# Identity products between token tiles, and the affine map that writes the rounded operand, in the first stage of a two-layer hybrid backbone

## The chip, the cores and the metric

The kernel runs on one core of a Trainium2 chip. Its five engines each work through a queue of their own: TensorE (matmuls and transposes, "PE" in the profile, with "PEld" its weight loads), VectorE ("DVE"), ScalarE ("ACT"), GpSimd ("POOL") and SyncE ("SP", which here only starts DMA transfers). Matmuls read SBUF and write PSUM; VectorE and ScalarE read both memories; GpSimd is used on SBUF alone here. The metric is the device time of one execution in microseconds (us).

## What is computed

Two layers over 512 latent tokens and 256 context tokens of width 1024. Every sub-layer normalises its input, modulates it, mixes it and adds it back:

```python
m_lat = jnp.split((sc @ mod_w[l] + mod_b[l])[:, None, :], 6, axis=-1)
m_ctx = jnp.split((scc @ mod_w[l] + mod_b[l])[None, None, :], 6, axis=-1)
h_ctx = _modulate(_rms(x_ctx, norm_pre_mix[l]), m_ctx[0], m_ctx[1])
h_lat = _modulate(_rms(x_lat, norm_pre_mix[l]), m_lat[0], m_lat[1])
...
def _rms(x, gain, eps=1e-6):
    xf = x.astype(jnp.float32)
    y = xf * lax.rsqrt(jnp.mean(xf * xf, axis=-1, keepdims=True) + eps)
    return (y * gain.astype(jnp.float32)).astype(x.dtype)
...
def _modulate(h, shift, scale):
    return h * (1 + scale) + shift
```

Here `sc` and `scc` are silu of the condition vectors, and `mod_w[l]` has 1024 rows and six column blocks of 1024. Layer 0 then projects h with `even_w_in`, runs gated linear attention beside grouped-query attention, projects the result out and applies a SwiGLU feed-forward; layer 1 does the same with an HGRN2 mixer. The change concerns only what comes first: norm and modulation of layer 0, and the first columns (288 of them: gate inputs and part of the queries) of its input projection.

## The kernel before

**Operands in two parts.** Large matmuls run on a rounded type (fp32r in the profile). To keep f32 accuracy each operand is split into H, the value rounded, and L, the remainder of value minus H, and a product is three matmuls (`mm3`): H by H, H by L, L by H. In most places ScalarE writes H as a cast and VectorE writes L as a subtraction (`put`, line 740, the operand x; `fetched`'s `split`, line 781, the weights wH and wL).

**The order.** A scheduler lays the instructions of each engine's queue in an order at build time, by priority in the text and by what it estimates to be ready. Instructions of TensorE that are made while `self.pinned` is set keep the order of the text. `issue_after(x)` adds an edge that keeps what is made inside it, where it is on x's own engine, behind x in that queue; other engines are not held. `behind()` (line 1543) does this for every instruction in `self.latest`. An engine works through its queue in order.

**The first stage**, in `run` (lines 1918 to 2037), is written out by hand:

- `constants` (line 373) makes the identity on GpSimd, starts the DMAs of some rows of constants on ScalarE's queue, and turns them with one transpose (pt_rows) into columns (col). From these ScalarE makes scT, silu of the conditions.
- `fetch` and `loads` start all the transfers on SyncE's queue: the six token tiles xt (two of context, 4 and 5, then four latent, 0 to 3), then for each quarter qd of the model width eight pieces of mod_w (mraw, 256 KB each, nine double-piece buffers) and 288 columns of the input projection (zraw).
- `turn(t)`, once for each token tile: ScalarE squares and sums (junk), VectorE makes ms, GpSimd raises it to -1/2 (rs), VectorE scales the tile in place (xt, line 1931), TensorE transposes its eight 128x128 blocks into a PSUM tile of which there are two buffers (line 358, xT), and ScalarE and VectorE copy one half each into xT in SBUF (line 1938).
- `sums(qd, ks)`: the two column blocks shift and scale of the modulation, for one quarter, as f32 matmuls with scT for weights, 32 output rows at a time (mod_acc). After the second half VectorE copies the sums (modrows); `cols(qd)` transposes them (modT), adds the bias (modcol) and makes the scale with the norm's gain (aff, line 1980).
- `apply(qd, r, t0, n)`: for the two 128-row blocks k of a quarter, the affine map scale by x plus shift in place on xT, then H and L of it into the operand x. The context (r = 1, 256 tokens) goes first, then the latents (512 tokens). The map is on ScalarE for latents where k % 4 is not 0 (line 1989), and on VectorE otherwise (line 1991); the cast is on ScalarE (line 743), the remainder on VectorE (line 744).
- `weights(qd)` splits that quarter's zraw (lines 783 and 784).
- `z(t0, qd, parts)`: the projection of two token tiles over that quarter's two blocks, accumulated in PSUM (nat).

TensorE's order is: the transposes of all six tiles, both halves of quarter 0's sums; then for each next quarter: projection of the context tiles over the quarter before, half the sums, one latent tile, the other half of the sums, the second latent tile, the transpose of the sums, the last two latent tiles. The last quarter's projections are made in the mixer that follows, ahead of its own projections (gqk).

Of the kernel before, what the change touches and what calls it, by code (L numbers as in the profile page):

```python
# [8 lines left out]
F32 = mybir.dt.float32  # L9
# [3 lines left out]
AF = mybir.ActivationFunctionType  # L13
# [4 lines left out]
P = 128  # L18
D = 1024
# [297 lines left out]
class Net:  # L317
# [3 lines left out]
    def __init__(self, ctx, tc, I, out):  # L321
# [4 lines left out]
        self.pinned = False  # L326
        self.turns, self.steps, self.pair, self.casts = [], [], [], []
        pool = lambda name, bufs=1, **k: ctx.enter_context(tc.tile_pool(name=name, bufs=bufs, **k))
# [28 lines left out]
    def tr(self, *a):  # L357
        return self.pin(self.nc.tensor.transpose(*a))

    def mm_tile(self, name):  # L360
        return self.ps.tile([P, 1024], F32, tag="mm", bufs=1 if self.narrow else 2, name=name)
# [10 lines left out]
    def constants(self):  # L372
        nc, I, cst = self.nc, self.I, self.cst
        self.ident = cst.tile([P, P], F32, name="ident")
        make_identity(nc, self.ident)
        self.scT = cst.tile([P, KD, 32], F32, name="scT")
        self.neghalf = cst.tile([P, 1], F32, name="neghalf")
# [12 lines left out]
            )  # L390
        )()

        nc.gpsimd.memset(self.scT, 0.0)
# [380 lines left out]
    def fetched(self, src, k, n, raw=None):  # L774

        nc = self.nc
        raw = self.wp.tile([P, WU], F32, tag="raw", bufs=3, name="raw") if raw is None else raw
        m = k * n
        nc.sync.dma_start(out=raw[:, :m].rearrange("p (k n) -> p k n", k=k), in_=src)

        def split(pool=None, to=None):
            H, L = to or [(pool or self.wp).tile([P, WU], F32R, tag=f"w{x}", bufs=4, name=f"w{x}") for x in "HL"]
            self.casts = self.casts[-1:] + [nc.scalar.copy(H[:, :m], raw[:, :m])]  # L783
            nc.vector.tensor_tensor(L[:, :m], raw[:, :m], H[:, :m].bitcast(F32), op=ALU.subtract)  # L784
            return H[:, :m].rearrange("p (k n) -> p k n", k=k), L[:, :m].rearrange("p (k n) -> p k n", k=k)

        return split
# [1111 lines left out]
    def run(self):  # L1899
# [19 lines left out]
        with self.pool("pre0") as pp:  # L1919
# [3 lines left out]
            def fetch(*ts):  # L1923
                for t in ts:
                    xts[t] = pp.tile([P, D], F32, tag="xt", bufs=6, name=f"xt{t}")
                    nc.sync.dma_start(out=xts[t], in_=xin(t))

            def turn(t):
                xt = xts.pop(t)
                rs = self.rstd(self.sumsq(xt), D)  # L1930
                nc.vector.tensor_scalar(xt, xt, rs, None, op0=ALU.mult)
                pt = self.mm_tile(f"xT{t}")
                for k in range(KD):
                    self.tr(pt[:, k * P : (k + 1) * P], xt[:, k * P : (k + 1) * P], self.ident)
                for hf in range(2):
                    dst = xT[:, hf * 4 : hf * 4 + 4, t * P : (t + 1) * P]
                    src = pt[:, 512 * hf : 512 * hf + 512].rearrange("p (k i) -> p k i", k=4)
                    (nc.vector.tensor_copy if hf else nc.scalar.copy)(dst, src)

# [44 lines left out]
            def apply(qd, r, t0, n):  # L1984
                tok = slice(t0 * P, (t0 + n) * P)
                for k in range(2 * qd, 2 * qd + 2):
                    x = xT[:, k, tok]
                    if r == 0 and k % 4:
                        nc.scalar.activation(x, x, AF.Identity, bias=B[:, r, k : k + 1], scale=A[:, r, k : k + 1])
                    else:  # L1990
                        nc.vector.tensor_scalar(x, x, A[:, r, k : k + 1], B[:, r, k : k + 1], op0=ALU.mult, op1=ALU.add)
# [267 lines left out]
```

## Time and profile before

| | us |
|---|---|
| median of 3 runs | 1679.83 (1679.76 to 1680.23) |
| the profiled execution, whole | 1680.5 |
| its span, first to last instruction | 1678.7 |
| TensorE busy in the span | 1640.6 |
| first stage, until the last projections over the last quarter end | about 56 |

The page gives shares of the whole span; a stage is read from the chain of work that ended last (which names, step by step, what the last instruction had to wait for), from the timeline and from the table of windows. In the chain's rows the first number is the start in us, the second the length, then engine, tile and line. Line 355 is the helper of every matmul and line 358 that of every transpose, so there the tile's name tells the step.

### The profile page before, as it was taken

Reading aid. Unit: us, or ns where it says so; the run is one execution under the profiler, and the core shown is the slowest. Engines: PE = TensorE matmul, PEld = TensorE weight load, DVE = VectorE, ACT = ScalarE, POOL = GpSimd, SP = SyncE. Lnnn points to the kernel's source line nnn. Section 1 sums busy time; section 2 is a strip of 40 time slices with the busy share of each in tenths; the row PEclk is TensorE's granted clock in tenths of the full one; section 3 lists DMA queues with packets and bytes.
Section 4 is the critical chain, followed back from the end, with each engine's and each line's share of the span. In section 5 each row is a group of like instructions: output and inputs, shape, how many; then the busy total and the mean of one; then the engine's idle time right before and its main releaser. Section 6 shows DMA issues by size and latency. Waiting matters only on the chain.

```text
span 1678.7 us, 32395 instructions
## 1 busy us (share of the span) xinstructions
PE 1640.6 (98%) x13347; PEld 1476.9 (88%) x13347; DVE 1313.0 (78%) x2104; ACT 917.4 (55%) x1560; POOL 121.6 (7%) x129
## 2 busy tenths in 40 slices
PE   6999998999999999999999999999999999999997
PEld 5899987888999999998887788888888899999886
DVE  4889768866898989768668648788775599987887
ACT  4745557846544443445447536566564565555654
POOL 1004210001000000002102000000000100000310
PEclk9999999999999999999999999999999999999999
DMA  9651002164253446249516542111114334333973
GB/s 336 187 154 42 2 28 101 52 197 152 92 150 102 133 149 193 79 134 223 101 54 210 194 132 64 52 54 50 52 56 159 126 107 120 114 101 101 227 162 138
DMA packets 184735, 204.77 MB, mean 122 GB/s; under 512 B 7142, under 2 KB 141836, under 8 KB 184588
## 3 DMA queue, kind: packets, MB, share of 16 engines
q1 hardware_dynamic: 173996, 181.98, 34.6%
q0 software_dynamic: 9024, 17.30, 5.8%
q10 hardware_dynamic: 1568, 3.43, 0.6%
q8 instruction: 104, 1.70, 0.4%
q14 instruction: 43, 0.35, 0.1%
HBM read 193.23 MB, written 9.46 MB: 121 GB/s over the span
## 4 chain that ended last, share of the span: by engine, by line
PE 82%; DVE 9%; DMA 4%; ACT 4%; issue 2%; POOL 0%; DVEq 0%; ACTq 0%; POOLq 0%
PE nat L355 12%; PE a L355 10%; PE ff L355 8%; PE E L355 7%; PE x L355 6%; PE oproj L355 6%; PE o L355 4%; PE b L355 3%; PE D L355 3%; PE fq L355 3%; PE gqk L355 2%; PE pearly L355 2%; PE q L355 2%; PE S L355 2%; PE poh L355 1%
## 5 line engine op out<-in xcount | busy, mean ns | idle before, releaser
L355 PE MATMUL nat<-wH,x 128*128 128x256 f32 (+2 forms) x968 | 227.6, 322 | 2.7 <-ACT x L743 2.5
L355 PEld LDWEIGHTS nat<-wH,x 128*128 128x128 f32 x968 | 162.7, 191 | 21.2 <-ACT x L743 3.9
L840 ACT CAST wH<-raw 128x1024 fp32r<-128x1024 f32 x120 | 124.8, 1050 | 101.6 <-DVE raw L865 39.2
L841 DVE TENSOR_TENSOR wL<-raw,wH 128x1024 fp32r<-128x1024 f32 x120 | 145.7, 1221 | 24.2 <-ACT wH L840 23.7
L355 PE MATMUL nat<-wL,x 128*128 128x256 f32 (+2 forms) x484 | 153.8, 318 | 1.8 <-DVE wL L784 1.8
L784 DVE TENSOR_TENSOR wL<-raw,wH 128x1024 fp32r<-128x1024 f32 x79 | 95.7, 1222 | 50.9 <-ACT wH L783 50.0
L355 PE MATMUL ff<-x,wH 128*128 128x512 f32 (+1 forms) x512 | 127.7, 340 | 0.0
L677 POOL TENSOR_TENSOR rs<-ms,neghalf 128x1 f32<-128x1 f32 (+2 forms) x62 | 63.3, 1025 | 787.7 <-DVE ms L675 787.6
L783 ACT CAST wH<-raw 128x1024 fp32r<-128x1024 f32 x79 | 82.1, 1049 | 68.6 <-PE ff L355 19.8
L355 PE MATMUL oproj<-wH,x 128*128 128x512 f32 x320 | 102.2, 394 | 0.5 <-ACT x L1310 0.4
L355 PEld LDWEIGHTS nat<-wL,x 128*128 128x128 f32 x484 | 92.3, 191 | 7.9 <-DVE wL L784 2.7
L355 PEld LDWEIGHTS ff<-x,wH 128*128 128x128 f32 x512 | 87.3, 190 | 10.0
L606 DVE SCALAR_TENSOR_TENSOR macc<-mraw,scT,macc 128x1024 f32<-128x1024 f32 x70 | 87.9, 1280 | 9.9 <-DMA mraw<-in_mod_w_dram 9.8
L355 PE MATMUL x<-wH,two 128*128 128x512 f32 x280 | 90.5, 392 | 0.9 <-DVE y L1831 0.7
L992 ACT COPY qkh<-arr 128x512 f32<-128x512 f32 x112 | 70.1, 642 | 36.4 <-DVE arr L997 32.2
L1753 POOL DMA_DIRECT2D t<-in_ffn_w_down_dram x36 | 41.8, 1199 | 639.6 <-DVE t L1792 337.5
L355 PE MATMUL ff<-x,wL 128*128 128x256 f32 (+1 forms) x256 | 86.2, 337 | 0.0
L865 DVE TENSOR_TENSOR raw<-raw 128x512 f32<-128x512 f32 x120 | 82.7, 689 | 2.8
L997 DVE TENSOR_TENSOR arr<-arr,f 128x512 f32<-128x512 f32 x112 | 74.2, 687 | 1.9 <-ACT qkh L992 0.3
L355 PEld LDWEIGHTS oproj<-wH,x 128*128 128x128 f32 x320 | 59.9, 188 | 13.1 <-ACT x L1310 1.1
L355 PE MATMUL E<-T,wH 128*128 128x384 f32 (+1 forms) x320 | 70.3, 309 | 0.4 <-DVE go L918 0.4
L355 PE MATMUL E<-x,wH 128*128 128x384 f32 (+1 forms) x320 | 70.7, 310 | 0.0
(422 smaller groups left out, 4538.1 us busy)
## 6 DMA issues: line engine op xcount, KB each, us to landing
mraw<-in_mod_w_dram SPq DMA_DIRECT2D x80, 512.0 KB, 4.3
raw<-in_ffn_w_gate_dram SPq DMA_DIRECT2D x44, 512.0 KB, 3.8
raw<-in_ffn_w_up_dram SPq DMA_DIRECT2D x44, 512.0 KB, 4.8
raw<-in_odd_w_in_dram SPq DMA_DIRECT2D x40, 512.0 KB, 3.7
t<-in_ffn_w_down_dram POOLq DMA_DIRECT2D x30, 512.0 KB, 7.9
raw<-in_ffn_w_down_dram SPq DMA_DIRECT2D x28, 512.0 KB, 7.3
mraw<-in_mod_w_dram SPq DMA_DIRECT2D x32, 256.0 KB, 6.3
raw<-in_even_w_in_dram SPq DMA_DIRECT2D x16, 512.0 KB, 5.0
```

What stands on the lines that cost most here:

```text
L355: return self.pin(self.nc.tensor.matmul(*a, **k))
L606: nc.vector.scalar_tensor_tensor(a, u, w, a, op0=ALU.mult, op1=ALU.add)
L677: nc.gpsimd.tensor_tensor(rs, ms, self.neghalf.to_broadcast([P, w]), op=ALU.pow)
L783: self.casts = self.casts[-1:] + [nc.scalar.copy(H[:, :m], raw[:, :m])]
L784: nc.vector.tensor_tensor(L[:, :m], raw[:, :m], H[:, :m].bitcast(F32), op=ALU.subtract)
L840: self.nc.scalar.copy(H, f)
L841: self.nc.vector.tensor_tensor(L, f, H.bitcast(F32), op=ALU.subtract)
L865: add = lambda o, x, y: nc.vector.tensor_tensor(o, x, y, op=ALU.add)
L992: nc.scalar.copy(qkv[:, :, :, half, :], dst)
L997: nc.vector.tensor_tensor(dst, dst, tb, op=ALU.mult)
L1753: add = lambda o, src: self.pin(nc.gpsimd.dma_start(out=o, in_=src, accum_op=ALU.add))
```

## The change

`warm(n)` issues n f32 products of the identity with itself into a PSUM tile (idle) that nothing reads. It is called 18 times over while the constants load, and with small counts between the token tiles, around the first sums and before the first affine map; the constants' TensorE instructions are pinned now.

The norm's VectorE instructions of a token tile (ms and the scaling of xt) are put behind the VectorE half of the copy of the tile two turns earlier, from the third tile on. The last tile's turn moves behind the first half of quarter 0's sums.

`apply` no longer writes the mapped value back: ScalarE writes H straight from xT with the affine map, for every k and both streams; VectorE computes the mapped value in f32 into a spare tile (xa, four buffers) and subtracts H from it.

`weights` makes its remainder on GpSimd, for all four quarters, and quarter 0's split is put behind the last tile's copies as the others are behind the last apply.

```diff
@@ Net @@
+    def warm(self, n):
+
+        for _ in range(n):
+            self.mm(self.idle, self.ident, self.ident, start=True, stop=True)
+
@@ constants @@
         make_identity(nc, self.ident)
+        self.idle = self.sc_tile("idle", 1)[:, :P]
+        self.pinned = True
+        self.warm(18)
         self.scT = cst.tile([P, KD, 32], F32, name="scT")
...
         )()
+        self.pinned = False
@@ fetched @@
-        def split(pool=None, to=None):
+        def split(pool=None, to=None, vector=nc.vector):
...
-            nc.vector.tensor_tensor(L[:, :m], raw[:, :m], H[:, :m].bitcast(F32), op=ALU.subtract)
+            vector.tensor_tensor(L[:, :m], raw[:, :m], H[:, :m].bitcast(F32), op=ALU.subtract)
@@ run @@
+            emptied = []
+
             def turn(t):
                 xt = xts.pop(t)
-                rs = self.rstd(self.sumsq(xt), D)
-                nc.vector.tensor_scalar(xt, xt, rs, None, op0=ALU.mult)
+                ss = self.sumsq(xt)
+                with ExitStack() as behind:
+                    if len(emptied) > 1:
+                        behind.enter_context(self.tc.issue_after(emptied[-2][1].ins))
+                    nc.vector.tensor_scalar(xt, xt, self.rstd(ss, D), None, op0=ALU.mult)
...
-                    (nc.vector.tensor_copy if hf else nc.scalar.copy)(dst, src)
+                    self.latest = [*self.latest[-1:], (nc.vector.tensor_copy if hf else nc.scalar.copy)(dst, src)]
+                emptied.append(self.latest)
...
             def apply(qd, r, t0, n):
                 tok = slice(t0 * P, (t0 + n) * P)
                 for k in range(2 * qd, 2 * qd + 2):
-                    x = xT[:, k, tok]
-                    if r == 0 and k % 4:
-                        nc.scalar.activation(x, x, AF.Identity, bias=B[:, r, k : k + 1], scale=A[:, r, k : k + 1])
-                    else:
-                        nc.vector.tensor_scalar(x, x, A[:, r, k : k + 1], B[:, r, k : k + 1], op0=ALU.mult, op1=ALU.add)
-                    self.latest = self.put(h, k, tok, x)
+                    H, L = h.hl(k, tok)
+                    a, b = A[:, r, k : k + 1], B[:, r, k : k + 1]
+                    f = pp.tile([P, SEQ], F32, tag="xa", bufs=4, name="xa")[:, : n * P]
+                    cast = nc.scalar.activation(H, xT[:, k, tok], AF.Identity, bias=b, scale=a)
+                    nc.vector.tensor_scalar(f, xT[:, k, tok], a, b, op0=ALU.mult, op1=ALU.add)
+                    self.mark = nc.vector.tensor_tensor(L, f, H.bitcast(F32), op=ALU.subtract)
+                    self.latest = cast, self.mark
 
             def weights(qd):
-                if qd == 0:
-                    zu[0] = zu[0]()
-                    return
                 with self.behind():
-                    zu[qd] = zu[qd]()
+                    zu[qd] = zu[qd](vector=nc.gpsimd)
...
-            for t in order:
+            for t, n in zip(order[:-1], (1, 2, 2, 3, 3)):
                 turn(t)
+                self.warm(n)
             sums(0, lo)
+            turn(order[-1])
+            self.warm(3)
             sums(0, hi)
             weights(0)
+            self.warm(2)
             cols(0)
+            self.warm(5)
             apply(0, 1, 4, 2)
             apply(0, 0, 0, 4)
```

More of the change, by code (lines that the diff above doesn't have):

```diff
@@ L326, in __init__ @@
         self.pinned = False
-        self.turns, self.steps, self.pair, self.casts = [], [], [], []
+        self.turns, self.steps, self.pair, self.casts, self.latest = [], [], [], [], []
         pool = lambda name, bufs=1, **k: ctx.enter_context(tc.tile_pool(name=name, bufs=bufs, **k))
```

## The prediction

> **What bounds the kernel now.** The page first: which engine fills the span, and which one fills the chain of work that ended last.
>
> ```profile
> PE 1640.6 (98%) x13347; PEld 1476.9 (88%) x13347; DVE 1313.0 (78%) x2104; ACT 917.4 (55%) x1560; POOL 121.6 (7%) x129
> ...
> PE 82%; DVE 9%; DMA 4%; ACT 4%; issue 2%; POOL 0%; DVEq 0%; ACTq 0%; POOLq 0%
> ```
>
> TensorE is the bound nearly everywhere, so a microsecond saved ahead of a TensorE-bound stretch should reach the end. The change lies in the first 56 us. The chain, asked for the start of the run, in order of time (start, length, what):
>
> ```profile
> 16.33 4.47 PE xT L358 x24
> 20.80 1.93 PE mod_acc L355 x64
> ...
> 23.86 0.17 DVE aff L1980
> ...
> 24.12 0.81 ACT xT L1989
> 24.93 0.30 ACT x L743
> ...
> 25.28 2.65 PE nat L355 x12
> 27.93 1.87 PE mod_acc L355 x32
> ...
> 33.39 0.17 DVE aff L1980
> ...
> 34.75 2.04 PE nat L355 x12
> 36.80 1.01 PE mod_acc L355 x32
> ...
> 41.35 0.17 DVE aff L1980
> ...
> 46.76 1.01 PE mod_acc L355 x32
> ...
> 49.30 0.17 DVE aff L1980
> ...
> 52.84 0.70 DVE x L744
> ...
> 53.59 2.79 PE nat L355 x19
> ```
>
> Read it as one turning stage (to 20.80), the first modulation sums (to 22.73), then four quarters, each from one aff to the next. Quarter one lasts 33.39 - 23.86 = 9.53 us, the second and third 7.95 us. Quarter one is slow because the same 12 projection matmuls take 2.65 us against 2.04, and the same 32 records of sums 1.87 against 1.01. The windows view names the cause (length, busy time and count of each engine, granted TensorE clock, DMA share, GB/s):
>
> ```profile
> 26.00:26.50 0.50, 0.50 (x5) 0.50 (x5) 0.43 (x2) 0.50 (x3) 0.00 (x0) 0.97 1.08 354
> 26.50:27.00 0.50, 0.50 (x4) 0.50 (x3) 0.50 (x2) 0.50 (x2) 0.00 (x0) 0.50 1.08 348
> 29.50:30.00 0.50, 0.50 (x9) 0.28 (x2) 0.00 (x0) 0.00 (x0) 0.00 (x0) 0.62 1.10 343
> 23.06:26.47 3.41, 1.52 (x8) 1.17 (x9) 2.85 (x11) 2.35 (x5) 0.00 (x0) 1.00 1.10 360
> ```
>
> The clock stands at half from about 26.47 (0.97 in that half microsecond) to 29.88 (0.62), 3.41 us. In the 3.41 us ahead of it TensorE was busy for 1.52 us (45%): it waited for the sums' copies and the first affine map.
>
> **The turning stage.** Rows of the timeline (start, length, engine, line, in brackets the idle time before and what ended it):
>
> ```profile
> 1.30 0.29 POOL masks.py:199 TENSOR_SCALAR_AFFINE_SELECT ident<-ident 128x128 f32<-128x128 f32 x1
> ...
> 7.81 0.45 PE L358 MATMUL pt_rows<-ident,rows 128*128 128x128 f32 x1 [7.81 <-DMA rows<-in_mod_b_dram]
> ...
> 8.06 3.68 PE L358 MATMUL xT<-ident,xt 128*128 128x128 f32 x16
> ...
> 9.83 0.21 ACT L394 ACTIVATE scT<-col 128x16 f32<-128x16 f32 x1
> ...
> 11.10 0.57 ACT L1938 COPY xT<-xT 128x512 f32<-128x512 f32 x1
> ...
> 11.90 0.15 DVE L675 TENSOR_SCALAR ms<-ss 128x1 f32<-128x1 f32 x1
> ...
> 12.20 0.55 POOL L677 TENSOR_TENSOR rs<-ms,neghalf 128x1 f32<-128x1 f32 x1 [0.99 <-DVE ms L675]
> ...
> 12.78 0.75 DVE L1931 TENSOR_SCALAR xt<-xt,rs 128x1024 f32<-128x1024 f32 x1 [0.73 <-POOL rs L677]
> 13.45 0.68 DVE L1938 COPY xT<-xT 128x512 f32<-128x512 f32 x1
> ...
> 14.19 1.97 PE L358 MATMUL xT<-ident,xt 128*128 128x128 f32 x8 [2.46 <-DVE ms L675]
> ...
> 16.81 0.69 DVE L1938 COPY xT<-xT 128x512 f32<-128x512 f32 x1 [0.54 <-ACT xT L1938]
> ```
>
> The first tile's copy has ScalarE's half at 11.10 but VectorE's only at 13.45, because a later tile's norm stands ahead of it and waits 0.73 us for GpSimd. With two PSUM buffers the third tile's transposes cannot start before 14.19. One tile's eight transposes take 1.97 us there. VectorE's half starts when ScalarE's ends (16.81).
>
> What the change does here. It puts each norm behind the VectorE copy of the tile two before it, so the first copy no longer waits for norms. The cost: the norm's chain, 1.63 us from ms to the end of xt (11.90 to 13.53), now starts only after a copy. Where ScalarE's first half lands is the unknown. The transposes of that tile are the first 8 of the 16 that start at 8.06, done by 9.9, and at 10.04 ScalarE is through with two latent norms and the small scT; its row of before is 11.10, behind one more norm; behind two more it would be about 12.3. I take 10.04: first copy done at 10.04 + 0.57 + 0.69 = 11.3, third tile's transposes at 11.3 + 1.63 = 12.95. The loop over two tiles is norm 1.63, transposes, ScalarE's half 0.59, VectorE's 0.69. With transposes at full clock, about 1.2 us (below), that is 4.1 us, 2.1 a tile at least; VectorE's own work a tile, 0.15 + 0.75 + 0.69, fits beside it. So: fifth tile turned at 17.2 to 18.4, three products, first half of the sums to 20.1, last tile's transposes to 21.2 (its norm is through by 19.4), three products, second half to about 22.8. Before: 22.73. **I cost the turning stage at nothing**: the early copy and the clock pay for the norms' later start and the fillers. Ends: 1.5 us gained (products hidden, copies earlier still), 2.3 us lost (ScalarE's half at 12.3).
>
> The products' price, and the other durations, from groups that keep shapes apart (busy us in all, mean ns of one):
>
> ```profile
> L355 PE MATMUL poh<-Sh,arr 128*128 128x128 f32 x96 | 12.0, 275 | 0.0
> ...
> L1989 ACT ACTIVATE xT<-xT,modcol,aff 128x512 f32<-128x512 f32 x6 | 4.9, 814 | 17.6 <-DVE aff L1980 17.6
> ...
> L736 ACT ACTIVATE hf<-hT,modcol,aff 128x256 f32<-128x256 f32 x24 | 12.2, 557 | 1.7 <-PE hT L358 1.7
> ...
> L744 DVE TENSOR_TENSOR x<-xT,x 128x512 fp32r<-128x512 f32 x8 | 5.4, 690 | 1.6 <-ACT x L743 1.4
> ...
> L1991 DVE TENSOR_SCALAR xT<-xT,aff,modcol 128x512 f32<-128x512 f32 x2 | 1.1, 541 | 0.0
> ...
> L1362 POOL TENSOR_TENSOR natq<-natq,rs 128x512 f32<-128x512 f32 x6 | 7.7, 1289 | 15.2 <-DVE natq L1361 15.0
> ```
>
> An f32 product of 128x128x128 is two records (32 calls of the sums are 64 records at 20.80). At full clock one takes 12.0/96 = 0.125 us, so a product 0.25 us and, with its tail, eight transposes 1.2 us; at half clock the transposes show 0.21 a record, so 0.43 a product. The first 18 start when the identity is there (1.30 + 0.29), and end between 6.1 (full) and 9.3 (half). The first real matmul waits until 7.81 for its DMA, so they are hidden unless all run at half clock; then col's copy, which stands ahead of a norm on VectorE, is up to 1.5 us late. I take them as hidden.
>
> Does the clock hold? Between the turns TensorE has about 1.2 + 0.6 busy of 2.1 us, well above the 45% after which it fell, and from the last turns to the projections the fillers close the holes. I take the clock as full from the turns on.
>
> [...]
>
> **The four quarters.** Removed: on ScalarE the affine map written back (0.81) and the cast behind it (0.30 until its first user starts); added: one map from xT to the rounded operand, on VectorE a second f32 map (0.54 for 512, 0.41 for 256) into a spare tile.
> - From aff to the first projection: before 24.03 to 25.28, 1.25 us. After: 0.05 + 0.56 (L736's shape) + 0.05, 0.66, and the five products (1.25, starting some 0.6 before aff's end) end at about the same time. **0.5 us gained.**
> - Clock in quarter one: 2.65 - 2.04 and 1.87 - 1.01. **1.5 us gained.**
> - At the start of the next quarters aff to projection is 1.19 us, mostly behind the projection still running; what can be won is the hole ahead of it (0.2 to 0.4) and the waits inside the 12 matmuls (2.04 against 1.75 by the 19 in 2.79). The remainder needs f (0.41), the rounded part (0.56) and the subtraction (0.42), so part of these waits stays. **0.45 us each for quarters two and three**, 0.1 inside quarter one; between nothing and 0.7 each.
> - The end. VectorE's eight instructions of the last quarter are 2 x (0.41 + 0.42 + 0.54 + 0.69) = 4.1 us, starts overlapping a little: the last remainder ends 3.9 us after aff, before 53.54 - 49.47 = 4.07. VectorE takes ScalarE's place as the limit. **0.2 us gained.**
> - GpSimd's remainders: 512 wide takes 1.29 us, 576 some 1.45. For the first it has from about 23.5 until the second matmul of the projection near 25; the others are needed a quarter later. Nothing, unless the first slips by over half a microsecond.
>
> DMA might take over: the engines are full until 40 us.
>
> ```profile
> 27.90 5.59 SPq L1950 DMA_DIRECT2D mraw<-in_mod_w_dram  x8
> ...
> mraw<-in_mod_w_dram SPq DMA_DIRECT2D x32, 256.0 KB, 6.3
> ```
>
> The last piece lands at about 33.5 + 6 = 39.5 and is used at 46.76; that bears a gain of up to 7 us.
>
> **Sum**: 0 + 0.5 + 1.5 + 0.1 + 2 x 0.45 + 0.2 = 3.2 us. What follows is bound by TensorE, so it shifts whole. The profiled execution took 1680.5 us, 1.8 of it around the span of 1678.7; the median of the runs is 1679.83, 0.67 less. Forecast 1677.3 for a run like the profiled one, **1676.6** for the median.
>
> **The rivals.**
> 1. *The turns gain too*: ScalarE's first half still earlier and the fillers all in waits. For it: two buffers are what holds 14.19 back. 1.5 us more, and the projections' waits gone (0.3 more a quarter): 5.3 us, 1674.5.
> 2. *The turns cost*: ScalarE's half at its old place 11.10 or later, the fillers (six products, 1.5 us, stand beside the sums) on the path. For it: the order of before. 1 to 2.3 us back: 1677.6 to 1679.
> [...]
> 4. *Slower*: VectorE's queue puts the copy of the tile just before ahead of a norm, since the new edge only says what a norm may not precede. Each turn is then a chain of norm 1.63, transposes 1.2, copies 1.3, 4.1 us, in place of 2.1. It decides once two turns are so; with all four, 6.9 us lost against 3.2 gained: 1683.5. Against it: VectorE's order of before runs what is ready, and ms is ready early.
>
> **How the numbers follow.** A measurement of this kernel can tell about 0.2%, 3.4 us, from no change. Forecast 0.50, with 2.2 to 4.6 us gained, half of it beyond that bound; first rival 0.24; second 0.14; third 0.06; slower 0.06. So faster 0.25 + 0.24 = 0.49, same 0.25 + 0.14 + 0.06 = 0.45, slower 0.06. The range goes from 6 us gained to 0.2 us: 1673.8 to 1679.6.
>
> **What would show it.** Granted clock 1.00 from 16 to 56 us, the first sums' 64 records in two halves ending near 22.8, projection at aff + 0.7, quarter one at 7.5 us, the last remainder near 50.4. It is wrong if the turns end over 1.5 us away from 22.8, if a half clock shows anywhere after 12 us, or if a later stage, with its queues newly ordered, gives back what arrives there.

## The result: slower by 2.5 us, and the profile after

| | kernel before | changed kernel |
|---|---|---|
| median of 20 runs each | 1679.73 us (1677.74 to 1681.39) | 1682.26 us (1679.38 to 1685.59) |
| ratio | | 1.0015, 95% interval 1.0009 to 1.0022 |
| profiled execution, its span | 1680.5, 1678.7 us | 1683.77, 1681.9 us |

The page of the changed kernel, the busy row and the shares of the chain that ended last:

```profile
PE 1647.9 (98%) x13425; PEld 1484.2 (88%) x13425; DVE 1311.9 (78%) x2106; ACT 915.6 (54%) x1554; POOL 127.4 (8%) x133
...
PE 83%; DVE 9%; DMA 3%; ACT 3%; issue 2%; POOL 0%; DVEq 0%; SPq 0%; ACTq 0%; POOLq 0%
```

TensorE is busy for 7.3 us more in 78 more records (39 products). VectorE and ScalarE are each busy for less than 2 us less. Shares of the whole span say nothing of where; the chain in order of time does (start, length, what):

```profile
12.49 0.47 ACT xT L1952
...
14.40 0.76 DVE xt L1945
15.30 1.78 PE xT L358 x8
...
24.55 1.01 PE mod_acc L355 x32
...
35.84 0.54 DVE xa L2006
36.38 0.34 DVE x L2007
36.77 1.19 PE nat L355 x7
...
52.48 4.47 PE nat L355 x31
57.02 1.18 PE gqk L355 x5
```

The chain of the kernel before has its first gqk here:

```profile
56.45 5.53 PE gqk L355 x24
```

The first sums end at 24.55 + 1.01 = 25.56, against 22.73 before: 2.8 us late. The first gqk starts at 57.02, against 56.45 in the kernel before, so the four quarters win back most of that and 0.57 us is left. The turning stage is the place, and the windows of it (length, busy time and count of PE, PEld, DVE, ACT and POOL, granted clock, DMA share, GB/s) show both things that happen there:

```profile
10.65:15.30 4.65, 0.00 (x1) 0.03 (x1) 1.65 (x4) 2.62 (x7) 0.55 (x1) 1.00 1.10 350
12.08:15.49 3.41, 0.19 (x2) 0.22 (x3) 1.84 (x4) 1.36 (x5) 0.55 (x1) 1.00 1.10 348
15.49:18.90 3.41, 3.41 (x18) 3.41 (x17) 1.83 (x5) 0.59 (x1) 0.82 (x2) 0.50 1.10 358
```

TensorE stands still from 10.65 to 15.30. From 15.49 to 18.90 its clock is granted at half (0.50); the 3.41 us ahead of that held 0.19 us of work. ScalarE's rows in the timeline tell why it stood still (start, length, engine, line, operation, in brackets the idle time before and what ended it):

```profile
9.91 1.06 ACT L694 ACTIVATE junk<-xt 128x1024 bf16<-128x1024 f32 x1 [0.15 <-DMA xt<-in_x_dram]
...
11.23 1.06 ACT L694 ACTIVATE junk<-xt 128x1024 bf16<-128x1024 f32 x1 [0.16 <-DMA xt<-in_x_dram]
...
12.28 0.21 ACT L403 ACTIVATE scT<-col 128x16 f32<-128x16 f32 x1
12.39 1.05 ACT L1952 COPY xT<-xT 128x512 f32<-128x512 f32 x2
12.98 0.69 DVE L1952 COPY xT<-xT 128x512 f32<-128x512 f32 x1 [3.73 <-ACT xT L1952]
13.59 0.14 DVE L684 TENSOR_SCALAR ms<-ss 128x1 f32<-128x1 f32 x1
13.81 0.55 POOL L686 TENSOR_TENSOR rs<-ms,neghalf 128x1 f32<-128x1 f32 x1 [5.55 <-DVE ms L684]
14.40 0.75 DVE L1945 TENSOR_SCALAR xt<-xt,rs 128x1024 f32<-128x1024 f32 x1 [0.66 <-POOL rs L686]
```

ScalarE's queue now holds all six squares (junk; the last two are shown) ahead of scT and of its halves of the first two copies. In the kernel before, a copy stood between the fifth square and the sixth:

```profile
10.04 1.06 ACT L685 ACTIVATE junk<-xt 128x1024 bf16<-128x1024 f32 x1
11.10 0.57 ACT L1938 COPY xT<-xT 128x512 f32<-128x512 f32 x1
11.56 1.06 ACT L685 ACTIVATE junk<-xt 128x1024 bf16<-128x1024 f32 x1
```

In the changed kernel VectorE's half waits 3.73 us for ScalarE's, the third tile's norm waits for that half, as the new edge orders, and the transposes start at 15.30.

### The profile page after: what moved, and what is told of

It reads as the page before. It is cut to its first block, busy times and chain, and to the rows that moved or that the text cites. A ratio compares the mean times of both kernels' runs of the same rounds, so it can differ in the third digit from the quotient of the medians.

```text
span 1681.9 us, 32570 instructions
## 1 busy us (share of the span) xinstructions
PE 1647.9 (98%) x13425; PEld 1484.2 (88%) x13425; DVE 1311.9 (78%) x2106; ACT 915.6 (54%) x1554; POOL 127.4 (8%) x133
## 4 chain that ended last, share of the span: by engine, by line
PE 83%; DVE 9%; DMA 3%; ACT 3%; issue 2%; POOL 0%; DVEq 0%; SPq 0%; ACTq 0%; POOLq 0%
PE nat L355 12%; PE a L355 10%; PE ff L355 8%; PE E L355 7%; PE x L355 7%; PE oproj L355 6%; PE o L355 5%; PE b L355 3%; PE D L355 3%; PE fq L355 3%; PE gqk L355 2%; PE pearly L355 2%; PE q L355 2%; PE S L355 2%; PE poh L355 1%
## 5 line engine op out<-in xcount | busy, mean ns | idle before, releaser
L355 PE MATMUL a<-T,wH 128*128 128x384 f32 (+1 forms) x320 | 70.6, 309 | 2.0 <-ACT qb L912 1.2
L355 PE MATMUL a<-x,dH 128*128 128x384 f32 (+1 forms) x320 | 70.4, 309 | 1.0 <-ACT go L922 0.6
```

The costliest lines, as they stand in the source:

```text
L355: return self.pin(self.nc.tensor.matmul(*a, **k))
```

## The experiments

In all diffs "-" is the changed kernel unless another is named. Each run's kernel was timed beside the kernel before; of each there is one trace. To compare traces, the start of the same matmul is taken in each against the first trace of the kernel before ("lag", the median of nine matmuls around the place); "half clock" lists the stretches behind the first rise of the clock and within the first 60 us in which the granted clock is 0.50. Ahead of that rise the windows view prints 1.00, but eight transposes took 1.97 us there in the kernel before, as they do at a granted clock of 0.50 (1.94 us in e9 at 15.47; 1.04 in e4 at 9.63). The first rise is at 19.64 us in the first trace of the kernel before and at 12.22 in e1, at 4.6 to 7.4 with the leading products and at 10.7 to 12.9 in e3, e6 and e10.

| run | median, us | ratio to before (95%) | lag at the first gqk | lag at the end | half clock |
|---|---|---|---|---|---|
| changed kernel | 1682.26 | 1.0015 (1.0009 to 1.0022) | +0.57 | +3.67 | 15.49 to 18.90 |
| e1 before | 1679.83 (one run) | | -0.13 | -0.27 | 15.64 to 19.05, 25.88 to 29.29 |
| e2 changed kernel | 1683.10 | 1.0015 (1.0006 to 1.0024) | +0.86 | +1.67 | 16.21 to 19.63 |
| e9 changed kernel | 1682.99 | 1.0021 (1.0011 to 1.0032) | +1.43 | +1.21 | 14.13 to 20.96 |
| e16 changed kernel | 1682.45 | 1.0014 (1.0005 to 1.0023) | +1.35 | +1.00 | 14.23 to 21.06 |
| e3 one leading product | 1681.41 | 1.0009 (1.0000 to 1.0018) | -1.46 | +0.91 | none |
| e4 squares behind copies | 1677.92 | 0.9989 (0.9980 to 0.9997) | -2.58 | -3.32 | none |
| e5 the map alone | 1679.39 | 1.0000 (0.9991 to 1.0009) | -1.15 | +0.21 | 15.56 to 18.97, 25.80 to 29.21 |
| e6 no products | 1680.19 | 1.0002 (0.9993 to 1.0011) | -1.76 | -2.20 | 14.12 to 17.53 |
| e10 no products | 1679.77 | 1.0000 (0.9990 to 1.0010) | -0.84 | -1.35 | 14.75 to 21.58 |
| e7 squares behind, remainders first | 1677.55 | 0.9988 (0.9979 to 0.9997) | -3.44 | -2.55 | none |
| e15 the same again | 1677.58 | 0.9986 (0.9977 to 0.9995) | -3.10 | -2.74 | 13.10 to 16.52 |
| e8 squares behind, 12 products at gqk | 1682.53 | 1.0016 (1.0007 to 1.0025) | +1.53 | +2.95 | 13.67 to 17.09 |
| e11 norms free | 1683.98 | 1.0029 (1.0018 to 1.0040) | +2.16 | +6.08 | 14.01 to 20.83 |
| e12 remainders on VectorE | 1682.38 | 1.0014 (1.0005 to 1.0024) | +1.40 | +3.99 | 13.85 to 20.67 |
| e13 before, 12 products at gqk | 1683.32 | 1.0013 (1.0004 to 1.0022) | +2.52 | +3.26 | 15.35 to 22.17 |
| e14 before, 24 products at gqk | 1686.55 | 1.0035 (1.0023 to 1.0048) | +5.19 | +6.43 | 26.41 to 29.83 |

The kernel before had medians of 1679.84 to 1680.07 beside these runs.

### The two kernels again (e1, e2)

No edit.

> The kernel before, unchanged, for a second profile: how far two executions of one kernel differ, stage by stage. If the 3 us that the changed kernel loses between 160 us and the end of its profile are a property of the changed kernel, this execution ends within 0.7 us of the first profile's span (1678.7) and its stages do not drift. If they are what executions of this kernel do anyway, it drifts by 1 us or more in the feed-forward stages (660 to 680 us, 1375 to 1415 us). The first projection over the second quarter stays at 34.75 within 1 us.

> The changed kernel, unchanged, for a second profile and a time on this chip. Theory A (the loss is in the turns: ScalarE's first copy stands behind all six squares, TensorE idles over 4 us, the clock halves): first sums end at 25.6 within 1 us, with a half clock of 3.4 us somewhere between 13 and 20 us; median 1.5 to 3.5 us above the kernel before. Theory C (the greater part is lost in the feed-forward stages): the gap at 160 us is under 1 us and the rest comes after 660 us again, at the same places.

The kernel before repeats itself to 0.3 us at both places, though its half clock falls at other times; between the two places the traces lie up to 0.7 us apart. The changed kernel is again late by the same order of things (half clock from 16.21), 0.86 us behind at the first gqk, and again loses more behind the first stage, but less of it and at other places.

### ScalarE's order (e4)

The square of a latent tile is held behind ScalarE's half of the copy four turns back, in the manner in which the change itself holds norms behind VectorE's:

```diff
-                ss = self.sumsq(xt)
+                with ExitStack() as behind:
+                    if len(emptied) > 3:
+                        behind.enter_context(self.tc.issue_after(emptied[-4][0].ins))
+                    ss = self.sumsq(xt)
```

> The squares of the last two latent tiles are put behind ScalarE's half of the first two tiles' copies; all products kept. ScalarE's queue is then four squares, scT, copy, square, copy, square. Theory A: first copy's VectorE half done near 11.2 in place of 13.7, no idle stretch of TensorE over 2.5 us, no half clock after 12 us, first sums end at 22.5 to 23.2, last projections of the first stage some 2.5 us earlier than in the changed kernel; total 2 to 3 us under the changed kernel, level with the kernel before or up to 1.5 us under it. Theory B: first sums end stays within 1 us of 25.6. Theory C: the stage is shorter but the total is not.

It took 1677.92 us, 4.3 less than the changed kernel and 2.15 less than the kernel before, which is more than was expected. The timeline of its turning stage:

```profile
9.75 0.22 ACT L403 ACTIVATE scT<-col 128x16 f32<-128x16 f32 x1
9.85 0.56 ACT L1955 COPY xT<-xT 128x512 f32<-128x512 f32 x1
10.32 1.05 ACT L694 ACTIVATE junk<-xt 128x1024 bf16<-128x1024 f32 x1
10.45 0.69 DVE L1955 COPY xT<-xT 128x512 f32<-128x512 f32 x1 [1.10 <-ACT xT L1955]
...
12.76 1.06 PE L358 MATMUL xT<-ident,xt 128*128 128x128 f32 x8 [1.65 <-DVE xt L1948]
...
14.84 1.06 PE L358 MATMUL xT<-ident,xt 128*128 128x128 f32 x8 [0.57 <-DVE xt L1948]
...
16.98 1.06 PE L358 MATMUL xT<-ident,xt 128*128 128x128 f32 x8 [0.41 <-DVE xt L1948]
```

ScalarE's first half stands at 9.85 in place of 12.39, the third tile's transposes at 12.76 in place of 15.30, and a tile takes 2.08 to 2.14 us. Eight transposes take 1.06 us; in the changed kernel they took 1.78, with the clock at half from 15.49. One edge on ScalarE accounts for all that the turning stage lost.

### What brings the order about (e3, e6, e10)

In e3 the 18 leading products are one; in e6 and e10 `warm` makes none of the 39.

```diff
-        self.warm(18)
+        self.warm(1)
```

```diff
-        for _ in range(n):
+        for _ in range(0):
```

> One identity product in place of the leading 18, everything else of the change kept; with it ScalarE's queue has its first copy behind five squares, as before the change. Theory A: first copy's VectorE half done near 12.4 in place of 13.7, first sums end near 24, stage and total some 1 to 1.5 us shorter than the changed kernel, although the first 16 transposes run at half clock again. Theory B (the norms' edge and the products between tiles cost the time whatever ScalarE's order is): within 0.5 us of the changed kernel. If the leading products are worth something by themselves, it is slower than the changed kernel.

> The changed kernel with all 39 identity products left out; the edge for the norms, the map and the GpSimd remainders stay. ScalarE's queue then has four squares, scT, a square, a copy, a square, a copy, as before. Theory (the loss is ScalarE's order in the turns, which the products bring about): first sums end by 22.7 or earlier, last projections end 1.5 to 3 us earlier than before, time 1676.9 to 1678.5. Rival (products are needed to hold the clock): a half clock of 3.4 us falls between 15 and 30 us and takes 1.5 us or more: 1679 to 1680.5. Second rival (the edge for the norms is what costs): turns end at 25 us as in the changed kernel, 1681 or more.

> The version without products a second time, since its trace was of its fastest run (1678.42 against a median of 1680.19). Theory (products are worth their place through the clock in the first stage): a half clock between 12 and 30 us, first stage 1 to 2.5 us longer than in the version with squares behind copies (whose gqk started at 53.9). Rival (the first stage is as short, 55 us or less, and the time goes behind it): lag at 57 us -1.5 or less, and lost by the end.

Both edits leave ScalarE's lines alone, and both change its order. ScalarE's timeline in e3:

```profile
9.88 1.06 ACT L694 ACTIVATE junk<-xt 128x1024 bf16<-128x1024 f32 x1
...
10.93 0.57 ACT L1952 COPY xT<-xT 128x512 f32<-128x512 f32 x1
```

This is the order of the kernel before; e6 and e10 have it too, with the first copy at 10.98 and 10.92. On TensorE the leading products end ahead of the DMA that the first transpose waits for, as the changed kernel's timeline has it:

```profile
1.64 5.99 PE L355 MATMUL idle<-ident 128*128 128x128 f32 x36 [1.64 <-POOL ident masks.py:199]
7.81 0.30 PE L358 MATMUL pt_rows<-ident,rows 128*128 128x128 f32 x1 [0.18 <-DMA rows<-in_mod_b_dram]
```

So products that cost TensorE nothing bring the late copies about through the scheduler: with 18 products ahead, the order that it lays out for ScalarE has the last two squares ahead of the copies. That it does so since it expects the transposes later is an inference; that the order turns on the leading products is what the two edits show (e3 keeps the other 21).

e3 took 1681.41 us, 0.9 to 1.7 less than the changed kernel (1682.26, and 1683.10 beside it), and still 1.3 more than the kernel before. Its first stage is 1.5 us shorter than before, but later TensorE stands still for what the profile shows no reason for:

```profile
149.97 0.73 PE L355 MATMUL gqk<-x,wH 128*128 128x512 f32 x2 [1.32 <-issue]
...
180.85 0.21 PE L355 MATMUL pcg<-qkg 64*32 64x32 f32 x1 [0.78 <-issue]
```

These two stops are 2.1 us. The other traces have at most 0.31 us of such stops between 145 and 185 us. The edit takes 34 matmul records out ahead of that place. Whether that is the cause was not tried.

e6 and e10 leave out every product and have the order of before on ScalarE. Their time is that of the kernel before (+0.25 and -0.26 us), 2.2 us above e4 (0.25 and -0.26 against -2.15). The windows of e10:

```profile
11.34:14.75 3.41, 1.18 (x10) 0.86 (x8) 2.16 (x5) 1.67 (x4) 0.88 (x2) 1.00 1.10 349
14.75:21.58 6.83, 5.63 (x50) 4.50 (x48) 4.28 (x8) 1.76 (x3) 1.31 (x3) 0.50 1.10 353
```

Behind 3.41 us with TensorE busy for 1.18 the granted clock is 0.50 for 6.83 us. At the first gqk that trace is 1.7 us behind e4's (-0.84 against -2.58); e6's, with 3.41 us at 0.50, is 0.8 behind. So the order of before without products doesn't reach e4, and both times lie in the range of the rival by which products are needed to hold the clock (1679 to 1680.5).

But this doesn't price the products, since e4 differs from e6 and e10 in ScalarE's order as well: its first copy stands behind four squares (9.85), theirs behind five. e3 has their order on ScalarE and 22 products, and its clock doesn't fall after its first rise at 12.86. It is no earlier at the first gqk (-1.46, against -1.76 and -0.84). Its third tile turns here:

```profile
13.84 1.07 PE L358 MATMUL xT<-ident,xt 128*128 128x128 f32 x8 [0.79 <-DVE xt L1945]
```

That is 1.08 us behind e4's 12.76, and at the first gqk e3 is 1.12 behind e4. Nearly all that separates these two traces there is the place of one square. Nor do the products hold the clock each time: e8 and e15 have the turning stage of e4 with all its products, and fell to half at 13.67 and 13.10. What the products are worth in time is not shown; the squares behind copies without products would tell, and were not run.

### The edge for the norms (e11)

```diff
-                    if len(emptied) > 1:
+                    if False:
```

> The changed kernel without the edge that holds a norm behind the copy of the tile two before; all else stays. VectorE then has all six norms ahead of the first copy, ScalarE's queue stays at six squares, scT, copies. Theory (in the changed kernel the edge does its work on VectorE, and ScalarE's order holds the copies): VectorE's first copy at 14.5 to 15.5 in place of 12.98, the third tile's transposes at 16 to 17 in place of 15.3, turns behind it shorter, since all norms are done: first sums end 25 to 26.5, time 1682 to 1683.5. Rival (the edge is what costs, since norms wait for copies): third tile's transposes no later than 15.3 and first sums end by 24: 1680.5 or less.

VectorE's first copy comes later still, and the transposes with it:

```profile
15.08 0.28 DVE L419 COPY col<-pt_rows 128x128 f32<-128x128 f32 x1
15.46 0.23 ACT L403 ACTIVATE scT<-col 128x16 f32<-128x16 f32 x1 [2.98 <-DVE col L419]
15.58 1.05 ACT L1952 COPY xT<-xT 128x512 f32<-128x512 f32 x2
16.18 1.29 DVE L1952 COPY xT<-xT 128x512 f32<-128x512 f32 x2 [0.81 <-ACT xT L1952]
16.93 1.97 PE L358 MATMUL xT<-ident,xt 128*128 128x128 f32 x8 [5.85 <-DVE xT L1952]
```

The edge does its work: without it col's copy stands behind six norms on VectorE, scT and ScalarE's copies wait for col, and the third tile turns at 16.93 in place of 15.30. Here VectorE's order was the limit. The time is 3.95 us over before, of which the changed kernel has 2.5 to 3.0 already, so the edge is worth some 1.0 to 1.4 us there. Both queues need holding, and the change holds one.

### The map and the remainders (e5, e12, e7, e15)

e5 is the kernel before with the new `apply` and nothing else. e12 is the changed kernel with the weights' remainders on VectorE:

```diff
-                    zu[qd] = zu[qd](vector=nc.gpsimd)
+                    zu[qd] = zu[qd]()
```

e7 and e15 are e4 with the 512 wide f maps held behind the context's second remainder:

```diff
-                    nc.vector.tensor_scalar(f, xT[:, k, tok], a, b, op0=ALU.mult, op1=ALU.add)
+                    with ExitStack() as behind:
+                        if r == 0:
+                            behind.enter_context(self.tc.issue_after(last[0].ins))
+                        nc.vector.tensor_scalar(f, xT[:, k, tok], a, b, op0=ALU.mult, op1=ALU.add)
...
+                    if r:
+                        last[:] = [self.mark]
```

> The kernel before with the new affine map and nothing else of the change: no products, no edge for the norms, remainders of the weights on VectorE. If the map itself is sound and only the turning stage spoils the change: the turns as before (first sums end at 22.7, half clock near 26 to 30 may come again), aff to first projection 0.7 in place of 1.25, each later quarter 0.1 to 0.45 shorter, the last one 0.3 to 0.5: 1.0 to 2.0 us less than before, 1678.0 to 1679.1. Rival (the map gains only where products hold the clock and the norms are moved): within 0.4 us of before, 1679.7 to 1680.5.

> The changed kernel with the four remainders of the weights on VectorE again (0.8 us each) in place of GpSimd (1.4 to 1.6 us each). Theory (nothing waits for them on either engine): within 0.5 us of the changed kernel at 57 us, 1682 to 1683.5. Rival one (VectorE is the bound of the quarters, so each remainder costs there): 0.5 to 0.8 us in three quarters, 1.5 to 2.4 us more: 1684 or more. Rival two (GpSimd's pass slows VectorE while both run): quarters 0.3 us shorter each, 1681.5 or less.

> The version with the squares behind copies (1677.92), and in each quarter VectorE's 512 wide f maps held behind the context's remainders, so that the second context remainder no longer waits 0.4 to 0.8 us for a map. Theory (that hole is why quarters two and three gained 0.09 and not 0.45): 0.2 to 0.4 us less in quarters two to four, 0.5 to 1.0 us in all: 1676.9 to 1677.4. Rival (the projection then waits for the 512 wide maps, which start later by as much): within 0.3 us of 1677.9.

> The version with the squares behind copies and the context's remainders first, again, to place it against before: 2.0 to 3.0 us below before if its first result holds (1677.0 to 1678.0); within 1.0 us of before if that was chance.

e5: the map shortens the first stage by 1.15 us, 0.4 of it ahead of the first quarter, where nothing was changed. The time is that of before within its interval (0.55 lower in the median), between what the two expectations had; in its trace the gain is given back near 775 us, where TensorE waits 1.15 us for VectorE. The half clock at 25.80 is there as before, so the 1.5 us in quarter one are not the map's.

e12: the first gqk is 1.40 us behind, as in e9 (1.43), whose half clock lies alike. With the remainders on GpSimd (1.58 us each in the changed kernel) the median is 1682.26 us, with them on VectorE (0.75 each in the kernel before) 1682.38: this part of the change does nothing for the time.

e7: the four aff rows, with first and last start, of the changed kernel and, behind it, of e7:

```profile
L1995 DVE SCALAR_TENSOR_TENSOR aff<-modcol,col x4: 162/163/164, 26.7 to 50.4; 128x4 f32<-128x4 f32 x4
```

```profile
L1998 DVE SCALAR_TENSOR_TENSOR aff<-modcol,col x4: 162/164/164, 23.6 to 46.3; 128x4 f32<-128x4 f32 x4
```

Three quarters take 22.7 us in place of 23.7. In the changed kernel VectorE runs a 512 wide map (xa, 0.54) between the two remainders of the context (the chain's rows at 35.84 and 36.38), and TensorE waits for the second. The timeline of e7 has the remainders side by side (0.91 for the two) and the latents' maps behind:

```profile
32.06 0.91 DVE L2013 TENSOR_TENSOR x<-xa,x 128x256 fp32r<-128x256 f32 x2
...
32.88 1.00 DVE L2012 TENSOR_SCALAR xa<-xT,aff,modcol 128x512 f32<-128x512 f32 x2
...
33.80 1.29 DVE L2013 TENSOR_TENSOR x<-xa,x 128x512 fp32r<-128x512 f32 x2
```

In the traces this is worth 0.5 to 0.9 us over e4 at the first gqk; in the medians, 2.39 and 2.26 us below before against e4's 2.15, it can't be told from nothing, and at the end the two traces are behind e4's (-2.55 and -2.74 against -3.32). Its medians are the lowest of those run. e4, e7 and e15 are each faster than the kernel before by an interval that leaves out 1, and so than the changed kernel.

### The later loss (e8, e9, e13, e14, e16)

The changed kernel's traces are 0.57 to 1.43 us late at the first gqk (mean 1.05), its medians 2.5 to 3.0 us. e8, e13 and e14 put a known delay there: identity products into the bank that gqk fills next. This also shifts a few instructions of the gate stage in the queues of ScalarE and VectorE.

```diff
+                for _ in range(12 if x == 0 else 0):
+                    self.mm(pt[:, :P], self.ident, self.ident, start=True, stop=True)
                 for g in groups:
```

> The version with the squares behind copies (1677.92), and twelve identity products, 3.0 us, ahead of the first gqk projection behind the first stage, into the bank that it fills next. Theory (the changed kernel loses 2 us more behind its first stage because what follows is reached later, out of step with its transfers): 4.5 us or more above 1677.9: 1682.4 or more. Rival (a late arrival shifts what follows as a whole): 3.0 us, 1680.5 to 1681.3; the further loss of the changed kernel is then not one of arrival.

> The changed kernel a third time, for a third trace of it. In the two traces so far the first gqk projection stood 0.6 and 0.9 us behind the kernel before, and the end 3.7 and 1.7 us. If the further loss belongs to the kernel: 0.4 to 1.2 us behind at 57 us and 2 us or more behind at the end, the slips at b<-x,wH near 665 us and at a<-x,dH near 1390 us again. If it is chance: behind at the end by no more than at 57 us, give or take 0.8.

> The kernel before, with twelve identity products (3.0 us at 0.125 us a record) ahead of the first gqk projection, so that all behind the first stage is reached later by a known amount. Theory (what stands behind the first stage loses more than the delay when it is reached later, as the three traces of the changed kernel suggest): 4 us or more above before, 1684 or more. Rival (a delay passes through as a whole, and further loss in a trace is chance): 2.5 to 3.0 above before, 1682.4 to 1683.1.

> The same with twenty-four products, 6.0 us. Theory (later arrival costs extra, by a share of the delay): 8 us or more above before, 1688 or more. Rival (a delay passes through as a whole): 5.5 to 6.0 above before, 1685.4 to 1686.1. If the extra is a fixed sum for any delay: 7 to 7.5, about 1687.

> The changed kernel beside the two delayed ones, for a fourth trace. First stage 0.5 to 1.5 us longer than in before, with one window of half clock or two behind the 4.6 us in which TensorE waits for the first copies; time 2.4 to 3.5 us above before. If a delay passes through as a whole in the two runs above, then its median should come to about 1 us above before, 1681, unless the windows' phase puts more into the first stage than the four traces show.

Twelve products put 2.7 us in (in e13 the lag goes from -0.17 ahead of them to 2.52), twenty-four 5.36. In the medians they cost 3.48 and 6.71, by the ratios 2.2 (0.7 to 3.7) and 5.9 us (3.9 to 8.1). Both medians fell between the forecasts. A delay passes through as a whole; what the medians have on top of it, 0.8 and 1.4 us, these runs can't tell from nothing. A loss that grows with the delay by a share (8 us or more for e14) lies at the edge of the interval and is unlikely.

e8 took 1682.53 us, 4.6 above e4, as the theory of a further loss had it (1682.4 or more). That doesn't settle it: its trace was 1.4 us behind e4's before the products came (-1.14 against -2.58), with a half clock that e4's trace hasn't. e9 was late at the first gqk by 1.43 us and at the end by 1.21, as the reading by chance had it. e16's trace is alike (1.35 and 1.00), but its median is 2.6 us above before, where a whole delay alone would have made it about 1681.

What the further loss is made of can be seen where it falls. VectorE's accumulation of a later modulation, in the timeline of the changed kernel and then of the kernel before:

```profile
649.50 1.54 SPq L597 DMA_DIRECT2D mraw<-in_mod_w_dram  x2
654.97 1.28 DVE L615 SCALAR_TENSOR_TENSOR macc<-mraw,scT,macc 128x1024 f32<-128x1024 f32 x1 [2.10 <-DMA mraw<-in_mod_w_dram]
...
666.30 0.48 ACT L912 COPY go<-a 128x384 f32<-128x384 f32 x1 [3.17 <-DVE zy L1724]
...
666.84 0.62 PE L355 MATMUL a<-T,wH 128*128 128x384 f32 x2 [0.86 <-ACT go L912]
```

```profile
649.74 5.71 SPq L588 DMA_DIRECT2D mraw<-in_mod_w_dram  x3
653.81 1.28 DVE L606 SCALAR_TENSOR_TENSOR macc<-mraw,scT,macc 128x1024 f32<-128x1024 f32 x1 [0.70 <-DMA mraw<-in_mod_w_dram]
```

The same transfer, started at the same point of the work, is used 5.47 us after its issue in one execution (654.97 - 649.50) and 4.07 in the other. VectorE is late by that, then the casts behind it, then a copy that TensorE waits for. Such slips stand at few places (665, 775, 1390 and 1661 us), in some traces and not in others: the changed kernel's first trace has 1.1 us at 665 and 1.9 near 1390 (there a cast of ScalarE waits 2.87 us for a transfer, 1.07 in the kernel before), its third (e9) has neither, though it is later at the first gqk. A slip of 0.8 us or more at 665 is in the changed kernel's first trace, e8, e11 and e12, four of the seven traces that are 0.5 to 2.2 us late at the first gqk. It is in none of the nine that are earlier there, and in neither of the two that are later (e13, e14).

Put together: the four profiled executions of the changed kernel took 1682.0 us in the mean, 1.5 above the profiled one of before, which itself took 0.4 to 0.8 more than the medians of its kernel. That makes 1.9 to 2.3 us, somewhat less than the 2.5 to 3.0 of the medians. Of it 1.05 us is in the first stage. Of the rest, what can be seen is the slips in the first two traces; e9 and e16 show none of this kind. Why the medians lie 1.5 to 2 us above what the first stage loses, and whether the changed kernel draws more slips than the kernel before by anything but chance, stays open.

## Why the prediction was wrong

The forecast was 1676.6 us, the range 1673.8 to 1679.6; it came out at 1682.26. Step by step, in us against the kernel before, read from the aff rows and the chains (the right-hand column is the version with ScalarE's and VectorE's order mended, e7):

| step | predicted | changed kernel | e7 |
|---|---|---|---|
| turning stage and first sums (first aff) | 0 | +2.9 | -0.25 |
| quarter one, with first projection and clock | -2.1 | -1.6 | -1.9 |
| quarters two and three | -0.9 | -0.2 | -0.8 |
| last quarter to gqk | -0.2 | -0.5 | -0.5 |
| sum at the first gqk | -3.2 | +0.6 | -3.4 |

Of the 5.7 us between forecast and time, 3.8 are in this table; the others lie behind the first stage.

- **The step that failed** is the turning stage, "I take 10.04". The text had the three places where ScalarE's first half could land, 10.04, 11.10 and "behind two more it would be about 12.3"; it landed at 12.39. What decided it was not weighed at all: ScalarE's order is laid out by the scheduler anew, and the 18 leading products, costed at nothing since TensorE waits there, moved it. An order taken over from the trace of before was treated as a fact of the new kernel. The stage was costed at nothing and took 2.9 us more; e4 and e7, with the first half at 9.85, took 0.25 less than before.
- **The second and third rival came together.** They stood as alternatives, with 0.14 and 0.06 (the third is a fall of the clock in the turns). In the changed kernel one stands behind the other: copies late by 2.5 us leave TensorE 4.65 us without work, and from 15.49 the clock is at 0.50. Against e4 the third tile is 2.54 us late (15.30 and 12.76), and from there to the end of the first sums it takes 10.26 us in place of 9.67 (25.56 - 15.30, 22.43 - 12.76), so the half clock's own price is 0.6 us in this trace. The third rival's price, some 2.5 us, was the author's estimate, and no run shows it. Even with both prices added (2.3 and 2.5 us) the forecast would have been 1681.4, since neither rival has a loss behind the first stage.
- **The clock in the turns.** "Full from the turns on" was wrong in the changed kernel. With the copies early it was right in e4 and e7 and wrong in e8 and e15, which have the same turning stage. The reason given, TensorE busy for 1.8 of 2.1 us in each turn, holds only once the turns run; the gap ahead of them was not counted.
- **The turning stage's own arithmetic was right.** Third tile at 12.95, 2.1 us a tile, first sums at 22.8: with ScalarE's half at 9.85 (e4) the third tile came at 12.76, tiles took 2.08 to 2.14, and in e7 the first aff stands 0.25 us ahead of before.
- **Hidden products.** In the changed kernel's first trace the 18 ended ahead of pt_rows, as predicted. In e4 and e9 they took 6.95 and 6.98 us in place of 5.99 (median record 421 ns in place of 275), and pt_rows came at 8.42 and 8.45; even so the copies were early in e4, since ScalarE came to them only at 9.85. As a load they cost nothing; as an entry in the scheduler's list they cost the turning stage.
- **Quarter one**: the clock's share came as predicted (in the changed kernel the granted clock was 1.00 from 26.50 to 33.00, and the 32 records of sums took 1.01 us in place of 1.87). Of the 0.5 us for the first projection little came: it starts 0.75 us after aff ends (27.65), as predicted, but then waits for the second remainder behind a 512 wide map.
- **Quarters two and three**: predicted 0.45 each "between nothing and 0.7", measured 0.1 each. The map's second copy on VectorE, which was priced for its length, also took a place in the queue. With that place mended 0.4 each.
- **The fourth rival**, the one on the slower side, was a different mechanism and didn't occur: VectorE's order was as the edge intended.
- **What follows "shifts whole"**: e13 and e14 bear that out as far as they can tell (0.8 and 1.4 us on top in the medians). What the prediction left out is that single transfers land over 1 us later in some executions (5.47 us from issue to use in place of 4.07, a wait of 2.87 us in place of 1.07) and that TensorE is late by 1.1 and 1.9 us behind these two.

## What to carry to other kernels

Where a scheduler lays out the queues, work that is free on its own engine can still reorder the others: after an edit read the order of every queue that feeds the edited stage, and pin with an edge each one that the argument rests on, not only the one that the edit names. The gap on TensorE was paid for twice in the changed kernel, 2.54 us as the wait and 0.6 us as the half clock behind it, so rivals that can come together are to be added up. When remainders or maps share a queue, look at their place as well as at their length: on VectorE a map of 0.54 us stood ahead of the remainder that the next matmul waited for, and with the remainders first three quarters took 22.7 us in place of 23.7.

## What the runs showed of the hardware

- **Half clock in the traces.** The granted clock was 0.50 for 3.41 us in the changed kernel (from 15.49), the kernel before (from 26.47), e6 (from 14.12), e8 (from 13.67) and e15 (from 13.10), and for 6.83 us in e9 (from 14.13), e10 (from 14.75) and e13 (from 15.35). In the 3.41 us ahead of these stretches TensorE was busy for 0.19 us (changed kernel), 1.52 (before), 0.84 (e6), 1.48 (e8), 1.38 (e15), 0.42 (e9), 1.18 (e10) and 1.13 (e13). In e4 a length of 3.40 us with 2.07 us of work (12.00 to 15.40) had a clock of 1.00 behind it. In the first 3.41 us of the long stretches TensorE was busy for 2.07 us (e9), 2.21 (e10) and 2.53 (e13), in the short ones for 3.08 (e6) or all 3.41 (changed kernel, before, e8, e15). The two parts of e9's stretch:

```profile
14.13:17.54 3.41, 2.07 (x10) 2.10 (x11) 2.17 (x4) 0.10 (x1) 0.95 (x2) 0.50 1.10 358
17.54:20.96 3.42, 3.42 (x18) 3.42 (x17) 1.84 (x4) 1.07 (x2) 0.55 (x1) 0.50 1.10 348
```

In the four traces of the changed kernel the half clock begins at 15.49, 16.21, 14.13 and 14.23 and lasts 3.41, 3.42, 6.83 and 6.83 us; the two traces with the longer stretch are 0.5 to 0.9 us later at the first gqk than the two with the shorter.
- **Transposes and the clock.** The clock first rose at 19.64 us in the first trace of the kernel before. In the 3.41 us ahead of that TensorE did nothing but f32 transposes, 3.31 us of them.
- **Stops with no releaser.** TensorE stood for 1.32 and 0.78 us in e3 (ahead of 149.97 and 180.85); the profile names only "issue". In the first trace of the kernel before the longest such stop between 145 and 185 us is 0.17 us.
